# Zeros under the low parts of the keys: the 64-row products of two attentions take 128 rows

## The chip, the cores and the metric

The kernel runs on one core of a Trainium2 chip. The metric is the time of one launch on the device in microseconds (us). TensorE is called PE below, its loads of the stationary operand PEld; VectorE is DVE, ScalarE ACT, GpSimd POOL, and SP issues most of the DMAs.

## What is computed

Two decoder blocks over 256 tokens of width 2048 in float32. The first has three attentions side by side (sparse A with an indexer, latent B with rotated key parts, C over a memory), the second a gated recurrence, a convolution and a feed forward. What the change touches is the indexer's score and the rotated part of B's logits; cut from the reference:

```python
def first_block(x, mem, positions, rel_bias, ...):
    h = rms_norm(x, norm_g[l])
    (aq, ak, av, az, iq, ik, iw, bcq, bckv, bkpe, bz, cq, cz, gates) = jnp.split(h @ w_in[l], IN_OFFSETS, axis=-1)
    ...
    iq = iq.reshape(bsz, seq, IDX_HEADS, IDX_DIM)              # 16 heads of 64; ik: 64 wide, one for all heads
    o_a = dsa_attention(aq, ak, av, iq, ik, iw, positions, rel_bias)   # the indexer's relu(iq . ik) picks 64 keys
    ...
    qb = jnp.concatenate([qb[..., :B_NOPE], apply_rope(qb[..., B_NOPE:], cos, sin)], axis=-1)   # 8 heads of 128 + 64
    kb = jnp.concatenate([kb[..., :B_NOPE], apply_rope(kb[..., B_NOPE:], cos, sin)], axis=-1)
    o_b = mla_attention(qb, kb, vb)                            # logits = qb . kb over 128 + 64
```

## The kernel before

**Exact products in pieces.** A number is held as a high part rounded to the type that PE takes in one pass (fp32r) and a low part that is the exact rest. A weight product is three products: high by high, low by high (both with the weights' high part, lines 292 and 293) and high by low (line 295). Weights arrive in chunks of two k tiles (512 KB); ACT makes the high part `wh` (line 277), DVE the low part `wl` (line 278), three chunks ahead of the products, and each chunk is 12 products of 512 columns on PE.

**One order for all.** The order of every engine is fixed when the program is built. `drive` (line 297) walks through the chunks, and after each chunk `side` (line 226) lets the generators of the attentions go one step. So the side work's products stand on PE between two chunks, and its vector work on DVE and ACT between two splits. How many steps a chunk gets is set by costs added up in `debt`, by the helpers `act`, `tt`, `ts`, `mm` and so on; a call straight to an engine adds nothing there.

**The indexer** (`gen_index`, line 752). Heads are 64 wide, so a query's high part lies on rows 0 to 63 of a tile `iqT` and its low part on rows 64 to 127. The key tile `ikT` has two planes: plane 0 has the key's high part twice (rows 0 to 63 and 64 to 127), plane 1 its low part on rows 0 to 63. One product over 128 rows with plane 0 gives high by high and low by high together; a second one over 64 rows adds high by low (lines 801 and 802):

```python
                    self.mm(p[:, i, :], x, ikt[:, 0, :ns], True, False)
                    self.mm(p[:, i, :], x[0:64], ikt[0:64, 1, :ns], False, True)
```

It runs for 16 heads and two token tiles: eight groups of two heads with 256 keys (four products between two chunks), then four groups of four heads with 128 keys (eight products).

**The rotated part of B** (`gen_B_half`, line 958, once for each half of the heads). `qn` and `kn` are the 128 plain channels in float32, one product in two recorded passes; `qp` holds the rotated query's high and low part, `kp` the rotated key's high part twice, `kpl` its low part on rows 0 to 63 (lines 1039 to 1041):

```python
                        self.mm(L[:, j, :ns], qn[:, h, c], kn[:, h, :ns], True, False)
                        self.mm(L[:, j, :ns], qp[:, h, c], kp[:, h, :ns], False, False)
                        self.mm(L[:, j, :ns], qp[0:64, h, c], kpl[0:64, h, :ns], False, True)
```

A group is two heads of one token tile: per half two groups with 128 keys and two with 256, in `attend` (line 412).

The functions, with the line numbers of the profile:

Of the kernel before, what the change touches and what calls it, by code (L numbers as in the profile page):

```python
# [9 lines left out]
F32 = mybir.dt.float32  # L10
# [10 lines left out]
NEG = 1e30  # L21
# [5 lines left out]
KG = 2        # k tiles of a weight chunk  # L27
RAW = 4       # weight chunks in flight from DRAM
LA = 3        # chunks split ahead of the products
NSLOT = 31    # 4 KiB slots  # L30
# [5 lines left out]
def thresholds():  # L36
    """Smallest distance of each T5 bucket."""
    return [0 if b == 0 else (b if b <= 16 else math.ceil(16 * 8 ** ((b - 16) / 16) - 1e-9))
            for b in range(32)]


def shape_constants():
    """Tables that depend on shapes alone."""
    c = {}
    c["k_ident"] = np.eye(P, dtype=np.float32)
    t = np.arange(P)
    tri = np.where(t[None, :] <= t[:, None], 0.0, -1.0).astype(np.float32)
    c["k_causal"] = np.concatenate([tri, np.zeros((P, P), np.float32), tri], 1)
    lev = []
    for i in range(7):  # L50
        lev.append(((t[:, None] >> (i + 1)) == (t[None, :] >> (i + 1)))
                   & ((t[:, None] >> i) != (t[None, :] >> i)))
    c["k_levels"] = np.stack(lev, 1).astype(np.int32)
    thr = np.array(thresholds(), np.float32)
    thr[0] = -NEG
    k5 = np.zeros((P, 8), np.float32)
    k5[:, 0] = np.tile(thr, 4)
    for b in range(4):
        k5[32 * b:32 * b + 32, 1 + b] = 1.0
    c["k_bucket"] = k5  # L60
    inv = np.float32(1) / np.power(np.float32(10000), np.arange(0, 64, 2, dtype=np.float32) / np.float32(64))
    c["k_freq"] = np.tile(inv.astype(np.float32)[None], (P, 1))
    return c


class Slots:
    """Hands out 4 KiB pieces of SBUF by hand."""
# [24 lines left out]
class Job:  # L92
    """One column block of a product: out[256 tokens, n] = x @ w[:, n0:n0+n]."""
# [8 lines left out]
class Builder:  # L102
# [56 lines left out]
    def mm3(self, out, a, b, start=True, stop=True):  # L159
        """(ah + al)^T (bh + bl) without the part below float32's last bit."""  # L160
        self.mm(out, a[0], b[0], start, False)
        self.mm(out, a[1], b[0], False, False)
        self.mm(out, a[0], b[1], False, stop)

    def split(self, hi, lo, src, g=None):
        """hi + lo = src (times g per partition), exactly."""
        if g is None:
            self.act(hi, src)
            self.tt(lo, src, hi.bitcast(F32), ALU.subtract)
        else:  # L170
            self.act(hi, src, AF.Copy, scale=g)
            self.stt(lo, src, g, hi.bitcast(F32), ALU.mult, ALU.subtract)
# [22 lines left out]
    def rstd(self, out, ss, width):  # L195
        """out = (ss / width + eps) ** -0.5, on a few columns."""
        n = self.cols(ss)
        t = self.work([P, 16], "rs_t", bufs=4)[:, :n]
        self.ts(t, ss, 1.0 / width, EPS, ALU.mult, ALU.add)
        self.debt["g"] += 2.0  # L200
        self.nc.gpsimd.tensor_tensor(out, t, self.cneg[:, :n], op=ALU.pow)  # L201

# [41 lines left out]
    def plan(self):  # L244
        """Cuts the jobs into weight chunks."""
        self.chunks, self.raws, self.whs, self.nd, self.ns = [], {}, {}, 0, 0
        for j in self.jobs:
            ks = j.ks
            for c in range(0, len(ks), KG):
                part = ks[c:c + KG]  # L250
                assert part == list(range(part[0], part[0] + len(part)))
                self.chunks.append((j, c // KG, part, c == 0, c + KG >= len(ks)))

# [28 lines left out]
    def products(self, i, outs, tiles):  # L282
        """The chunk's products for some token tiles."""
# [13 lines left out]
    def drive(self):  # L297
# [20 lines left out]
        # the last chunks, one token tile after the other  # L318
# [8 lines left out]
    def gen_T(self, src, hi, lo, g=None, ev=None, free=(), nk=4, pause=False):  # L327
        """Transposes token-major [128, nk*128] pairs into hi + lo, times g per channel."""
# [34 lines left out]
    def hilo(self, nk, name):  # L363
        """hi and lo parts of x^T, four k tiles to a slot."""
        hs = [self.slots.get([P, 4, 256], F32R, f"{name}h{i}") for i in range(nk // 4)]
        ls = [self.slots.get([P, 4, 256], F32R, f"{name}l{i}") for i in range(nk // 4)]
        return hs, ls
# [5 lines left out]
    def head_ss(self, out, src, groups, width):  # L373
        """out[128, groups] = sums of squares of src[128, groups, width]."""
        sq = self.work([P, 768], "sq", bufs=1)[:, :groups * width].rearrange("p (g w) -> p g w", g=groups)
        self.act(sq, src, AF.Square)
        self.red(out, sq)

# [1 line left out]
    def attend(self, rounds):  # L380
# [30 lines left out]
        def s3(r):  # L411
            pt, nst = r.pop("PT"), r["ns"] // P
            if r["dv"] == 256:   # in two parts where the rows are long enough to gain from it
# [44 lines left out]
    def constants2(self):  # L458
        """Everything small that is not needed at once."""
# [53 lines left out]
        # causal masks of the indexer's scores  # L513
# [3 lines left out]
        self.ts(self.causal, self.causal, NEG)     # 0 or -NEG from here on  # L517
        yield 1
        # rope: angle = k * 2 pi + r with |r| <= pi, in exact parts
# [24 lines left out]
        # tables with the norm's gains: out = x * ct + swapped x * sw  # L544
# [14 lines left out]
        # positions relative to the first, exact in float32  # L559
# [14 lines left out]
        # pos_t - threshold, for (t % 4, bucket) on partitions and t // 4 along  # L574
# [5 lines left out]
        # differences of neighbouring buckets' biases, block diagonal over t % 4  # L580
# [13 lines left out]
    def warm(self):  # L594
        """Keeps the tensor engine's clock up until the first operands are in; gets ScalarE's table."""
# [14 lines left out]
    def gen_in(self, src, name, g0, r, hs, ls, at, every):  # L610
        """Loads a [256, 2048] input and transposes it, times the norm's gain; r = its rstd."""
# [32 lines left out]
    def gen_cT(self, blk, tag, g, dst, ev):  # L644
        """Heads' norm of one block (2 heads of 256) and its transpose, in two parts."""
# [60 lines left out]
    def gen_bias(self):  # L706
        """bias[t, h, s] from steps at the buckets' thresholds: 16 tokens' rows (t, h) at a time."""
# [4 lines left out]
        # through DRAM the rows change from (t, h) on partitions to t on partitions  # L712
        dram = [self.pd.tile([8 * P, P * (i + 1)], F32, name=f"biasd{i}", tag=f"biasd{i}") for i in range(2)]

        def steps(u):
            """0/1 steps of 4 or 2 groups of 16 tokens, two of their four parts to a tile."""
# [35 lines left out]
    def gen_index(self):  # L752
# [11 lines left out]
        # rows 0-63 and 64-127: hi and lo of the queries; hi twice, and lo, of the keys  # L764
        ikt = sl.get([P, 2, 256], F32R, "ikT")
        self.act(ikt[:, 0, :], p[:, :256])
# [23 lines left out]
        for tt in (1, 0):  # L790
# [6 lines left out]
            def s0(r):  # L797
                p = self.ps().rearrange("p (j s) -> p j s", j=nh)
                for i, h in enumerate(r["h"]):
                    x = iqT[h // 4][:, (h // 2) % 2, h % 2, tt * P:(tt + 1) * P]  # L800
                    self.mm(p[:, i, :], x, ikt[:, 0, :ns], True, False)
                    self.mm(p[:, i, :], x[0:64], ikt[0:64, 1, :ns], False, True)
# [21 lines left out]
        # the 64 largest of each row, ties to the lower index  # L824
# [14 lines left out]
    def gen_head128(self, blk, nh, dst, g, off=0):  # L839
        """Norm over heads of 128 and transpose: blk [128, 2, .] -> dst[128, nh, 256] times g."""  # L840
# [27 lines left out]
    def gen_A(self):  # L868
# [12 lines left out]
        # rows outside the selection go far below the others  # L881
# [26 lines left out]
    def gen_lat(self):  # L908
        """Transposed latents, and the rotated shared key part."""
# [48 lines left out]
    def gen_B_half(self, half, ct, sw, bc):  # L958
# [3 lines left out]
        # rotated parts: hi and lo of a query's head on rows 0-63 and 64-127; of the keys hi twice, and lo  # L962
# [34 lines left out]
        kpl = sl.get([P, 4, 256], F32R, "bkpl")  # L997
        for i in range(2):
# [33 lines left out]
        for i in range(2):  # L1032
            for t in range(2):
                def logits(L, i=i, t=t):
                    ns = P * (t + 1)
                    for j in range(2):
# [4 lines left out]
                        self.mm(L[:, j, :ns], qp[0:64, h, c], kpl[0:64, h, :ns], False, True)  # L1041
# [8 lines left out]
    def block1(self):  # L1050
# [12 lines left out]
        def begin():  # L1063
            self.warm()
            next(gmem)          # transposes
            self.gains0()
            next(gmem)          # first half
# [165 lines left out]
        # residual  # L1233
# [23 lines left out]
    def x_next(self, x, cb, ssp, r, store, g, name):  # L1257
        """After a residual block: sums of squares, the transposed parts for the next product."""
# [19 lines left out]
    # The lower bounds of the gates are c - c[0:1] over the layers; with one layer that is zero by  # L1278
    # shape, which leaves log f = log_sigmoid(z) and k = 1 - f = sigmoid(-z).
    def gen_hgrn(self, hf):  # L1280
# [4 lines left out]
        # -log f = L - min(z, 0) and -log k = L + max(z, 0), L = log(1 + exp(-|z|)); L passes through Q and K  # L1285
# [51 lines left out]
        # the diagonal  # L1337
# [18 lines left out]
        for li in range(8):  # L1356
# [21 lines left out]
            else:  # L1378
# [4 lines left out]
                for t in range(2):   # keys of tile 1 - t, queries of tile t  # L1383
# [271 lines left out]
    def finish(self, t):  # L1655
        """The last norm of one token tile."""
# [58 lines left out]
```

## Time and profile before

| | |
|---|---|
| timed runs | 2283.58, 2286.21, 2288.13 us; median 2286.21 |
| profiled execution | span 2284.2 us from first to last instruction; no other time of it is given |
| PE busy | 2259.6 us (99% of the span), 10514 products |
| PEld busy | 1882.4 us (82%), as many loads |
| DVE, ACT, POOL busy | 1317.7 us (58%), 1106.9 us (48%), 367.7 us (16%) |
| 16 DMA engines | 58.1% of their time on the main queue, 181 GB/s |
| granted clock of PE | 0.996 of 2.4 GHz over the span |

A busy PE is not PE at its peak: a product's recorded end is modelled, and products overlap in the pipe. What a product costs is read from the distance between its start and the next one's start.

### The profile page before, as it was taken

What the parts mean: (1) busy time and instruction counts of PE and PEld (TensorE: products, weight loads), DVE (VectorE), ACT (ScalarE), POOL (GpSimd) and SP (SyncE); (2) the same over time, 40 slices, a digit from 0 to 9 for tenths busy, and PEclk for the clock granted to TensorE, in tenths of its full rate; (3) what the DMA queues carried; (4) which work ended last, traced back from release to release, by engine and by line L of the source; (5) the groups of instructions that cost most, each with busy time, mean ns of one, the idle gap of its engine ahead of it and who ended that gap; (6) DMA issues with size and microseconds to landing.
All of it is one profiled execution on the core that took longest, in us unless ns stands there. A gap on an engine that the chain in (4) does not pass through costs nothing.

```text
span 2284.2 us, 27699 instructions
## 1 busy us (share of the span) xinstructions
PE 2259.6 (99%) x10514; PEld 1882.4 (82%) x10514; DVE 1317.7 (58%) x1457; ACT 1106.9 (48%) x1410; POOL 367.7 (16%) x299
## 2 busy tenths in 40 slices
PE   9989999999999999999999999999999999999998
PEld 7878878888888888888888888888888888888886
DVE  5744657655756555555675786555445544545545
ACT  5634535555655454444554654544444433444434
POOL 2093102200404101000263352000000000000001
PEclk9999999999999999999999999999999999999999
DMA  8545546555655556566655555566666666666664
GB/s 275 185 150 184 164 134 184 174 167 171 188 156 177 166 175 194 185 202 197 194 161 157 166 169 160 185 187 186 193 187 191 187 192 196 209 192 188 190 193 140
DMA packets 214933, 413.99 MB, mean 181 GB/s; under 512 B 13538, under 2 KB 20304, under 8 KB 214800
## 3 DMA queue, kind: packets, MB, share of 16 engines
q1 hardware_dynamic: 211936, 405.98, 58.1%
q0 software_dynamic: 2256, 5.19, 0.7%
q8 instruction: 82, 1.34, 0.2%
q10 hardware_dynamic: 608, 1.06, 0.1%
q14 instruction: 51, 0.42, 0.0%
HBM read 408.51 MB, written 3.67 MB: 180 GB/s over the span
## 4 chain that ended last, share of the span: by engine, by line
PE 77%; issue 14%; POOL 1%; DMA 0%; ACT 0%; DVE 0%; ACTq 0%; POOLq 0%; DVEq 0%
PE acc L292 24%; PE acc L293 23%; PE acc L295 23%; PE sp L157 4%; PE sp L177 2%; DMA gf<-in_final_norm_w_dram 0%; POOL x L132 0%; POOL bpt L132 0%; POOL ho L132 0%; ACT x L128 0%; DVE x L132 0%; POOL bpe L132 0%; POOL rs L201 0%; ACT zs L128 0%; ACT wh L277 0%
## 5 line engine op out<-in xcount | busy, mean ns | idle before, releaser
L278 DVE TENSOR_TENSOR wl<-raw,wh 128x1024 fp32r<-128x1024 f32 (+4 forms) x765 | 982.3, 1292 | 807.1 <-ACT wh L277 802.5
L277 ACT ACTIVATE wh<-raw 128x1024 fp32r<-128x1024 f32 (+4 forms) x765 | 801.1, 1053 | 873.8 <-PE acc L293 846.0
L292 PE MATMUL acc<-wh,xh 128*128 128x512 f32 (+2 forms) x864 | 342.2, 396 | 0.0
L293 PE MATMUL acc<-wh,xl 128*128 128x512 f32 (+2 forms) x864 | 336.6, 390 | 0.0
L292 PE MATMUL acc<-wh,h3h 128*128 128x512 f32 x704 | 274.8, 390 | 0.0
L293 PE MATMUL acc<-wh,h3l 128*128 128x512 f32 x704 | 273.9, 389 | 0.0
L295 PE MATMUL acc<-wl,xh 128*128 128x512 f32 (+2 forms) x864 | 230.3, 388 | 0.0
L292 PE MATMUL acc<-wh,h2h 128*128 128x512 f32 x512 | 202.2, 395 | 0.0
L293 PE MATMUL acc<-wh,h2l 128*128 128x512 f32 x512 | 199.4, 390 | 0.0
L295 PEld LDWEIGHTS acc<-wl,xh 128*128 128x128 f32 x864 | 162.6, 188 | 32.9
L292 PEld LDWEIGHTS acc<-wh,xh 128*128 128x128 f32 x864 | 162.9, 189 | 32.4
L293 PEld LDWEIGHTS acc<-wh,xl 128*128 128x128 f32 x864 | 163.0, 189 | 30.9
L295 PE MATMUL acc<-wl,h3h 128*128 128x512 f32 x704 | 188.2, 389 | 0.0
L295 PEld LDWEIGHTS acc<-wl,h3h 128*128 128x128 f32 x704 | 132.1, 188 | 27.4
L293 PEld LDWEIGHTS acc<-wh,h3l 128*128 128x128 f32 x704 | 132.2, 188 | 27.2
L292 PEld LDWEIGHTS acc<-wh,h3h 128*128 128x128 f32 x704 | 132.2, 188 | 27.1
L295 PE MATMUL acc<-wl,h2h 128*128 128x512 f32 x512 | 136.9, 389 | 0.0
L292 PE MATMUL acc<-wh,ah 128*128 128x512 f32 x344 | 134.0, 390 | 0.0
L293 PE MATMUL acc<-wh,al 128*128 128x512 f32 x344 | 133.8, 389 | 0.0
L295 PEld LDWEIGHTS acc<-wl,h2h 128*128 128x128 f32 x512 | 96.1, 188 | 20.0
L293 PEld LDWEIGHTS acc<-wh,h2l 128*128 128x128 f32 x512 | 96.2, 188 | 18.9
L292 PEld LDWEIGHTS acc<-wh,h2h 128*128 128x128 f32 x512 | 96.2, 188 | 18.9
(459 smaller groups left out, 2801.1 us busy)
## 6 DMA issues: line engine op xcount, KB each, us to landing
raw<-in_w_in_dram SPq DMA_DIRECT2D x328, 512.0 KB, 3.7
raw<-in_w_gate_up_dram SPq DMA_DIRECT2D x176, 512.0 KB, 4.2
raw<-in_w_down_dram SPq DMA_DIRECT2D x88, 512.0 KB, 4.2
raw<-in_w_out_dram SPq DMA_DIRECT2D x64, 512.0 KB, 4.2
raw<-in_w_branch_dram SPq DMA_DIRECT2D x48, 512.0 KB, 4.0
raw<-in_w_mem_kv_dram SPq DMA_DIRECT2D x31, 512.0 KB, 4.7
raw<-in_w_in_dram SPq DMA_DIRECT2D x8, 464.0 KB, 3.4
raw<-in_w_in_dram SPq DMA_DIRECT2D x8, 448.0 KB, 3.5
```

The source lines that it names most:

```text
L157: self.nc.tensor.matmul(out, lhsT, rhs, start=start, stop=stop)
L177: self.nc.tensor.transpose(out, in_, self.ident if k == P else self.ident[:k, :k])
L277: self.nc.scalar.activation(wh[:, k], r[:, k], AF.Copy)
L278: self.nc.vector.tensor_tensor(wl[:, k], r[:, k], wh[:, k].bitcast(F32), op=ALU.subtract)
L292: self.nc.tensor.matmul(outs[t], a, wh[:, kk], start=first and kk == 0, stop=False)
L293: self.nc.tensor.matmul(outs[t], b, wh[:, kk], start=False, stop=False)
L295: self.nc.tensor.matmul(outs[t], a, wl[:, kk], start=False, stop=last and kk == len(ks) - 1)
```

## The change

Of the comments only their text is gone. Three things change in the program:

```diff
@@ gen_index
         ikt = sl.get([P, 2, 256], F32R, "ikT")
+        self.nc.vector.memset(ikt[64:128, 1, :].bitcast(F32), 0.0)
         self.act(ikt[:, 0, :], p[:, :256])
         self.tt(ikt[0:64, 1, :], p[0:64, :256], ikt[0:64, 0, :].bitcast(F32), ALU.subtract)
@@ gen_index, s0
                     self.mm(p[:, i, :], x, ikt[:, 0, :ns], True, False)
-                    self.mm(p[:, i, :], x[0:64], ikt[0:64, 1, :ns], False, True)
+                    self.mm(p[:, i, :], x, ikt[:, 1, :ns], False, True)
@@ gen_B_half
         kpl = sl.get([P, 4, 256], F32R, "bkpl")
+        self.nc.vector.memset(kpl[64:128].bitcast(F32), 0.0)
         for i in range(2):
@@ gen_B_half, logits
                         self.mm(L[:, j, :ns], qp[:, h, c], kp[:, h, :ns], False, False)
-                        self.mm(L[:, j, :ns], qp[0:64, h, c], kpl[0:64, h, :ns], False, True)
+                        self.mm(L[:, j, :ns], qp[:, h, c], kpl[:, h, :ns], False, True)
```

The second product of a head now streams a key plane of 128 rows, whose lower 64 rows are zero, against the whole query tile. The zeros are written once for the indexer and once for each half of B. Every engine's order stays as it was, but for these three writes on DVE. The first, in the indexer (`iw` are the heads' weights, `wl` the splits of the weight chunks):

```order
 L137 TENSOR_SCALAR iw<-mA 128x32
 L278 TENSOR_TENSOR wl<-raw,wh 128x1024 x2
+L766 MEMSET ikT 64x256
 L132 TENSOR_TENSOR ikT<-sp,ikT 64x256
 L278 TENSOR_TENSOR wl<-raw,wh 128x1024
```

It comes just ahead of the write of the low part. In B it stands further ahead, on DVE before the first key norm of a half (`ss` are the sums of squares of the keys' heads, `rs_t` goes to POOL for the power, `bkn` and `bkpl` are the key tiles; numbers in names differ since there is one instruction more):

```order
 L132 TENSOR_TENSOR bqp<-sp,bqp 64x256 x2
-L146 TENSOR_REDUCE ss_5203<-sq 128x4
-L132 TENSOR_TENSOR ss_5203<-ss_5203,skpe 128x4
-L137 TENSOR_SCALAR rs_t<-ss_5203 128x4
+L999 MEMSET bkpl 64x1024
+L146 TENSOR_REDUCE ss_5205<-sq 128x4
+L132 TENSOR_TENSOR ss_5205<-ss_5205,skpe 128x4
+L137 TENSOR_SCALAR rs_t<-ss_5205 128x4
 L278 TENSOR_TENSOR wl<-raw,wh 128x1024 x5
 L137 TENSOR_SCALAR bkn<-sp,vT 128x512
 L132 TENSOR_TENSOR bkpl<-sp,bkp 64x256 x2
```

Only the line of the zeros is new there; what stood behind stands one instruction later. It is the same in the second half.

## Rows read from the trace of the kernel before

**Rows 1.** The page's head and part 1: busy us (share of span) xinstructions.

```profile
span 2284.2 us, 27699 instructions
...
PE 2259.6 (99%) x10514; PEld 1882.4 (82%) x10514; DVE 1317.7 (58%) x1457; ACT 1106.9 (48%) x1410; POOL 367.7 (16%) x299
```

**Rows 2.** Who PE waited for, whole span: total us, times, longest us.

```profile
PE sp L177 <- POOL cq L132: 4.0, 2, 3.5
```

**Rows 3.** Instructions on tiles ikT and bkpl: ns min/median/max, first and last start, forms.

```profile
L157 PE MATMUL sp<-ikT,iqT x64: 220/328/385, 279.7 to 336.4; 128*128 128x256 f32 x16, 64*128 64x256 f32 x16, 128*128 128x128 f32 x16, 64*128 64x128 f32 x16
...
L132 DVE TENSOR_TENSOR ikT<-sp,ikT x1: 405/405/405, 248.2 to 248.2; 64x256 fp32r<-64x256 f32 x1
...
L157 PE MATMUL sp<-bkpl,bqp x16: 324/352/384, 635.6 to 778.7; 64*128 64x128 f32 x8, 64*128 64x256 f32 x8
```

**Rows 4.** Timeline of PE, indexer, 256 keys: start us, us, instruction, shapes, count.

```profile
279.68 1.21 PE L157 MATMUL sp<-ikT,iqT 128*128 128x256 f32 x4
...
281.16 0.40 PE L293 MATMUL acc<-wh,xl 128*128 128x512 f32 x1
```

**Rows 5.** Timeline of PE and PEld behind that group.

```profile
280.83 0.50 PE L292 MATMUL acc<-wh,xh 128*128 128x512 f32 x1
280.82 0.19 PEld L292 LDWEIGHTS acc<-wh,xh 128*128 128x128 f32 x1
```

**Rows 6.** Timeline of PE and PEld, C's logits: twelve 128-row products, 256 columns.

```profile
261.82 0.28 PE L157 MATMUL sp<-ckT1h,cqT1h 128*128 128x256 f32 x1
...
263.14 0.19 PEld L292 LDWEIGHTS acc<-wh,xh 128*128 128x128 f32 x1
...
263.49 0.40 PE L293 MATMUL acc<-wh,xl 128*128 128x512 f32 x1
```

**Rows 7.** Timeline of PE, indexer, 128 keys.

```profile
334.74 2.01 PE L157 MATMUL sp<-ikT,iqT 128*128 128x128 f32 x8
...
337.02 0.39 PE L293 MATMUL acc<-wh,xl 128*128 128x512 f32 x1
```

**Rows 8.** Timeline of PE, B's logits with 128 keys, one group of two heads.

```profile
635.18 0.38 PE L157 MATMUL sp<-bkn,bqn 128*128 128x128 f32 x2
...
636.87 0.40 PE L293 MATMUL acc<-wh,xl 128*128 128x512 f32 x1
```

**Rows 9.** Timeline of PE, B's logits with 256 keys, one group of two heads.

```profile
642.10 0.59 PE L157 MATMUL sp<-bkn,bqn 128*128 128x256 f32 x2
...
644.44 0.40 PE L293 MATMUL acc<-wh,xl 128*128 128x512 f32 x1
```

**Rows 10.** Timeline of PE, A's logits: two float32 products of 128, then of 256 columns.

```profile
444.25 0.60 PE L157 MATMUL sp<-akT,aqT 128*128 128x128 f32 x4
...
444.93 0.40 PE L293 MATMUL acc<-wh,ucl 128*128 128x512 f32 x1
...
450.61 1.02 PE L157 MATMUL sp<-akT,aqT 128*128 128x256 f32 x4
...
451.70 0.40 PE L293 MATMUL acc<-wh,xl 128*128 128x512 f32 x1
```

**Rows 11.** Chain that ended last, in order of time: start, us, what.

```profile
631.06 1.53 PE sp L177 x14
```

**Rows 12.** Busy time by engine in a stretch: us, PE, PEld, DVE, ACT, POOL, PEclk, DMA.

```profile
279.00:315.00 36.00, 36.00 (x161) 27.42 (x160) 22.29 (x33) 16.70 (x22) 0.00 (x0) 1.00 0.47 140
```

**Rows 13.** Groups by line on DVE: a write of a constant; busy us, mean ns.

```profile
L597 DVE MEMSET warm<- 128x512 f32 x1 | 0.5, 485 | 0.1
```

**Rows 14.** Timeline of DVE, POOL and PE where B's second half makes its keys.

```profile
731.32 4.34 DVE L278 TENSOR_TENSOR wl<-raw,wh 128x1024 fp32r<-128x1024 f32 x3
...
734.54 2.72 POOL L132 TENSOR_TENSOR bpe<-kr,rs 128x128 f32<-128x128 f32 x2
...
736.78 1.07 PE L295 MATMUL acc<-wl,uah 128*128 128x512 f32 x4
...
740.41 0.60 PE L177 MATMUL sp<-ident,ukv 128*128 128x128 f32 x4
```

## The prediction

> **What bounds the kernel now.** I read the page's first part first: PE is busy 2259.6 of 2284.2 us [rows 1]. Next, whom PE waited for: eight entries over the whole span, the largest 4.0 us behind POOL [rows 2], and none of them in the stretches that the change touches. In the indexer PE is busy for all of its 36.00 us while DVE has 22.29 and ACT 16.70 [rows 12]. So PE sets the pace, and what a product costs has to be read from the starts on PE's timeline, since recorded ends overlap. The forms on the two key tiles then give the number of products that change: 32 in the indexer and 16 in B, 48 in all, 24 of 256 columns and 24 of 128 [rows 3].
>
> I measure each group of side products in one way: from its first start to the start of the second weight product (line 293) behind it. That takes in what the group does to the first weight product after it.
>
> - Indexer, 256 keys: 128 and 64 rows in turn, four products. 281.16 - 279.68 = 1.48 us [rows 4].
> - Attention C's logits: twelve products of the same 256 columns and the same type, all over 128 rows. 263.49 - 261.82 = 1.67 us [rows 6].
>
> A weight product of 512 columns takes about 0.23 us from start to start when nothing is in its way, so C's twelve cost 1.67 - 0.23 = 1.44 us, **0.12 us each**. The indexer's four cost 1.48 - 0.23 = 1.25 us, 0.31 each. Half of the four have half the rows, and they run at well under half the speed. C's products also add up three times into one PSUM region, so that is not what slows the indexer's. What differs is the change between 128 and 64 rows. The trace shows how: behind the group the load of the next stationary operand starts at 280.82 and its product at 280.83 [rows 5]. The load is not done ahead, during the product before, and its own product starts with it. Behind C's products the same load starts at 263.14, and the product it belongs to only 0.12 us later, 0.23 before 263.49 [rows 6]. So each step between 64 and 128 rows, in either direction, empties the pipe, and the exposed load and the emptying are paid 48 times on the way in and 48 times on the way out.
>
> **The change, part by part.**
>
> *The indexer with 256 keys, eight groups.* All products are now over 128 rows, the form of C's, so I take C's 0.12. A group then costs 4 x 0.12 + 0.23 = 0.71 us instead of 1.48: 0.77 us less, 8 times, **6.2 us**.
>
> *The indexer with 128 keys, four groups of eight products.* Before: 337.02 - 334.74 = 2.28 us [rows 7]. The trace has no fp32r product of 128 columns over 128 rows in a run of its own. From above the 0.12 of 256 columns bounds it; from below its half, 0.06, if columns alone counted. Nearest are the transposes, also 128 columns behind a load each: 14 in 1.53 us [rows 11], 0.11 us each. I take 0.11, because the load of the stationary operand has the same 128 columns in each case. A group is then 8 x 0.11 + 0.23 = 1.11 us: 1.17 less, 4 times, **4.7 us**.
>
> *B with 128 keys, four groups (two heads each).* Before: 636.87 - 635.18 = 1.69 us [rows 8]. The float32 part stays; A's logits have two such products alone, 444.93 - 444.25 = 0.68 us with the 0.23 [rows 10]. Two 128-row products for each of two heads add 4 x 0.11. After: 0.68 + 0.44 = 1.12, 0.57 less, 4 times, **2.3 us**.
>
> *B with 256 keys, four groups.* Before: 644.44 - 642.10 = 2.34 us [rows 9]. After: 451.70 - 450.61 = 1.09 [rows 10], plus 4 x 0.12 = 0.48, makes 1.57: 0.77 less, 4 times, **3.1 us**.
>
> *The zeros.* Three writes on DVE, over 64 partitions. DVE wrote 512 columns in 485 ns [rows 13]; in proportion that is 0.24 us for the 256 columns of `ikT` and 0.97 us for the 1024 of `bkpl`, 2.2 us in all. I cost them at nothing on the path. The indexer's low part, just behind its zeros, is written at 248.2, and the first product that reads it starts at 279.7 [rows 3]. In B two things are queued behind the zeros on DVE. One is the weight splits: that of 731.32 is one of three in 4.34 us, done about 1.2 us later, and PE takes it at 736.78 [rows 14], some 4.2 us to spare. The other is the keys' norm, which POOL waits for: its last step ends at 734.54 + 2.72 = 737.26 and PE transposes the keys at 740.41 [rows 14], 3.1 us to spare. Both exceed 0.97 us. If that cover were gone, the three writes would cost 2.2 us. A wait of the writes on an older user of their slots costs nothing either: the zeros come ahead of work that POOL itself waits for, so they can only wait for what POOL had done before.
>
> *Who is late next.* Over the 36 us of [rows 12] PE gets some 6 us faster; DVE then has 22.3 of about 30 us and ACT 16.7, and DMA, at 0.47 of its time, moves the same bytes in five sixths of the time. None comes to its limit, so what PE saves reaches the end. Later waits of PE, on POOL and on splits, follow PE's own pace, and no side chain with a wait spans one of the changed groups.
>
> **Sum.** 6.2 + 4.7 + 2.3 + 3.1 = 16.3 us, against the span of 2284.2: 2267.9. The execution that was profiled has only its span as a time; the median of the runs lies 2.0 us above it, and I take the same for the changed kernel: 2286.2 - 16.3 = **2269.9 us**. With 0.06 for the 48 products of 128 columns the saving is 18.7, with 0.12 it is 15.8, and with all zeros on the path as well 13.6.
>
> **The rivals.**
>
> *Nothing changes (the rows are not the cause).* If the 0.31 us came from the operands or from the place in the program, the 128-row form would cost what the 64-row form does, and with the zeros hidden the time stays at 2286. For it speaks that the 128-row products in the same groups are as slow as the 64-row ones. Against it: C's twelve, with the same type, columns and accumulation, and B, where other tiles show the same excess. The Trainium skill, page "TensorE: Matmul & The Clock Gate", section "Why this matters for your kernels", says that a single product over 32 rows takes the time of one over 128; by that rule alone this change would give 2286. The rule holds for a lone product and leaves out what the step between two row counts costs, which [rows 5] show here.
>
> *Slower: time goes with the rows.* If a 64-row product were cheap for its rows and a second half of rows were paid again, each of the 48 would double: 24 x 0.31 + 24 x 0.26 = 13.7 us more (0.26 is (2.28 - 0.23) / 8 from [rows 7]), 2299.9 us. The place is PE's stream of these groups, and it decides from the point where a 128-row product in an unbroken run costs more than 0.31 or 0.26 us. C's cost 0.12, so little speaks for it. The Trainium skill, page "TensorEngine Tiling (Array Packing)", section "Theoretical Speedup", promises up to a factor of two for a contraction of 64 rows or less, which would speak against the change; it needs two such products side by side, and all 48 here sit on rows 0 to 63, one after the other.
>
> *Half of the gain is given back.* PE comes sooner to the next chunk and waits for its split, or for POOL's key norm. From a saving of 16.3, a new wait of 0.5 us behind each of 16 of the 20 groups leaves 8: 2278 us. Against it stand the 4.2 and 3.1 us to spare above.
>
> **How the numbers follow.** Forecast 0.92, half given back 0.03, no change 0.03, slower 0.02. About 0.2% (4.6 us) is what a measurement of this kernel can tell from no change. Both of the first two are faster than that: 0.95; same 0.03; slower 0.02. The range goes from the largest saving (18.7) less the 2.6 us by which the fastest run lies under the median, 2265.0, to the smallest (13.6) plus the 1.9 us of the slowest run, 2274.5; the rivals outside it hold less than 2 in 10.
>
> **What would show it.** Right: four-product groups of the indexer at 0.71 us and eight-product groups at 1.11 by the same measure; all their products 128 rows; loads ahead of their products again; B's groups at 1.12 and 1.57; zeros of 0.24 and 0.97 us on DVE, and no new entry in PE's list of waits. Wrong: the products still 0.26 to 0.31 us apart, a wait of PE behind a split or POOL near 616 or 740 us, or an unchanged span with shorter groups.

## The result: 2269.9 us, 0.7% faster

The changed kernel takes 2269.93 us (median, 2268.29 to 2271.32) against 2285.64 us before (2283.58 to 2288.13): a ratio of 0.9933, 95% interval [0.9921, 0.9945], or 15.7 us less. The forecast was 2269.9 us within 2265.0 to 2274.5. The profiled execution spans 2266.4 us; its run took 2268.29 us, so 1.9 us lie around the span.

The page of the kernel after, head and part 1, answers to [rows 1]:

```profile
span 2266.4 us, 27702 instructions
...
PE 2243.3 (99%) x10514; PEld 1877.0 (83%) x10514; DVE 1318.7 (58%) x1460; ACT 1106.0 (49%) x1410; POOL 368.8 (16%) x299
```

The number of products is the same; PE is busy 16.3 us less, as much as the forecast's sum. DVE has three instructions more and is busy 1.0 us longer. The products on the two key tiles, as in [rows 3], now have no form with 64 rows:

```profile
L157 PE MATMUL sp<-ikT,iqT x64: 220/278/362, 278.5 to 324.7; 128*128 128x256 f32 x32, 128*128 128x128 f32 x32
...
L157 PE MATMUL sp<-bkpl,bqp x16: 275/277/282, 623.6 to 761.7; 128*128 128x128 f32 x8, 128*128 128x256 f32 x8
...
L766 DVE MEMSET ikT<- x1: 272/272/272, 247.2 to 247.2; 64x256 f32 x1
```

The timeline of PE and PEld after, for the same four kinds of group, in the order of [rows 4, 7, 8, 9], with the first load behind the first group:

```profile
278.47 0.64 PE L157 MATMUL sp<-ikT,iqT 128*128 128x256 f32 x4
...
278.82 0.19 PEld L292 LDWEIGHTS acc<-wh,xh 128*128 128x128 f32 x1
...
278.94 0.40 PE L292 MATMUL acc<-wh,xh 128*128 128x512 f32 x1
279.17 0.40 PE L293 MATMUL acc<-wh,xl 128*128 128x512 f32 x1
...
312.97 1.00 PE L157 MATMUL sp<-ikT,iqT 128*128 128x128 f32 x8
...
314.10 0.40 PE L293 MATMUL acc<-wh,xl 128*128 128x512 f32 x1
...
623.31 0.38 PE L157 MATMUL sp<-bkn,bqn 128*128 128x128 f32 x2
...
624.43 0.40 PE L293 MATMUL acc<-wh,xl 128*128 128x512 f32 x1
...
629.66 0.59 PE L157 MATMUL sp<-bkn,bqn 128*128 128x256 f32 x2
...
631.22 0.40 PE L293 MATMUL acc<-wh,xl 128*128 128x512 f32 x1
```

From the first start to the second weight product the groups take:

| group | count | before | forecast | after | saved, all groups |
|---|---|---|---|---|---|
| indexer, 256 keys | 8 | 1.48 | 0.71 | 0.70 | 6.2 |
| indexer, 128 keys | 4 | 2.28 | 1.11 | 1.13 | 4.6 |
| B, 128 keys | 4 | 1.69 | 1.12 | 1.12 | 2.3 |
| B, 256 keys | 4 | 2.34 | 1.57 | 1.56 | 3.1 |

That is 16.2 us. Behind the group the load now starts at 278.82, ahead of its product at 278.94; before, both started together [rows 5].

The two profiled spans differ by 17.8 us. Some 1.2 us of that are not of the change: the first touched group starts at 278.47 instead of 279.68, since PE waited 3.1 us instead of 4.0 for POOL's `cq` far ahead of it and a little less for the first operands. PE's waits after, the same eight entries; the largest answers to [rows 2]:

```profile
PE sp L177 <- POOL cq L132: 3.1, 2, 2.4
...
PE acc L292 <- ACT wh L277: 1.7, 1, 1.7
...
PE sp L177 <- DMA ident<-in_k_ident_dram: 0.9, 1, 0.9
```

No wait of PE behind a split or behind POOL is new, so the zeros stay covered: the work queued behind them is done before PE needs it. The tightest place is the keys' norm in B's second half, where POOL's last step ends at 720.97 + 2.72 = 723.69 and PE transposes it as the second of two, at about 726.37:

```profile
720.97 2.72 POOL L132 TENSOR_TENSOR bpe<-kr,rs 128x128 f32<-128x128 f32 x2
...
726.26 0.38 PE L177 MATMUL sp<-ident,bpe 128*128 128x128 f32 x2
```

That leaves 2.7 us behind one write of zeros. Over the indexer's stretch PE stays busy throughout while the other engines move closer to it, as in [rows 12]:

```profile
279.00:315.00 36.00, 36.00 (x190) 30.89 (x190) 25.74 (x36) 19.54 (x25) 0.00 (x0) 1.00 0.55 175
```

DVE went from 22.29 to 25.74 of 36 us, DMA from 0.47 to 0.55. No engine is at its limit, so the time saved reaches the end.

### The profile page after: what moved, and what is told of

It reads as the page before. It is cut to its first block, busy times and chain, and to the rows that moved or that the text cites. A ratio compares the mean times of both kernels' runs of the same rounds, so it can differ in the third digit from the quotient of the medians.

```text
span 2266.4 us, 27702 instructions
## 1 busy us (share of the span) xinstructions
PE 2243.3 (99%) x10514; PEld 1877.0 (83%) x10514; DVE 1318.7 (58%) x1460; ACT 1106.0 (49%) x1410; POOL 368.8 (16%) x299
## 4 chain that ended last, share of the span: by engine, by line
PE 77%; issue 15%; POOL 1%; DMA 1%; ACT 0%; DVE 0%; ACTq 0%; POOLq 0%; DVEq 0%; SPq 0%
PE acc L292 23%; PE acc L293 23%; PE acc L295 23%; PE sp L157 4%; PE sp L177 2%; DMA xres<-in_x_dram 0%; DMA gf<-in_final_norm_w_dram 0%; POOL x L132 0%; ACT wh L277 0%; POOL ho L132 0%; POOL bpt L132 0%; ACT x L128 0%; POOL bpe L132 0%; DVE wl L278 0%; POOL rs L201 0%
```

## Experiments

Two questions stayed open after the result. Is it the step between row counts that cost, or are a 64-row product or these key tiles slow by themselves? And is the writing of zeros free, or was it only small?

### Each place alone

The indexer's products over 128 rows, B's as before; and the other way round:

```diff
 # e1_index_only, against the changed kernel
-        self.nc.vector.memset(kpl[64:128].bitcast(F32), 0.0)
-                        self.mm(L[:, j, :ns], qp[:, h, c], kpl[:, h, :ns], False, True)
+                        self.mm(L[:, j, :ns], qp[0:64, h, c], kpl[0:64, h, :ns], False, True)
 # e2_b_only, against the changed kernel
-        self.nc.vector.memset(ikt[64:128, 1, :].bitcast(F32), 0.0)
-                    self.mm(p[:, i, :], x, ikt[:, 1, :ns], False, True)
+                    self.mm(p[:, i, :], x[0:64], ikt[0:64, 1, :ns], False, True)
```

> The indexer's second products take 128 rows, B's stay at 64. If each place pays for its own steps between 64 and 128 rows, the indexer's twelve groups alone give 8 x 0.77 + 4 x 1.14 = 10.7 us: about 2274.9 us, ratio to the kernel before 0.9953. The groups then read 0.71 and 1.13 us, B's stay at 1.69 and 2.34 us. If the gain came from one place, or from the start of the kernel (where the two profiles also differ by over 1 us), it is either all 15.7 us (2269.9) or none (2285.6).

> Only B's third products take 128 rows, the indexer's stay at 64. If each place pays for its own steps, B's eight groups give 4 x 0.57 + 4 x 0.78 = 5.4 us: about 2280.2 us, ratio 0.9976, and with the indexer alone the two sum up to the whole change. If B's products hide behind something else, or the zeros of 0.91 us twice are on the path, it is 0 to 3.6 us.

Measured: the indexer alone 2275.33 us, ratio 0.9952 [0.9939, 0.9964]; B alone 2279.55 us, ratio 0.9973 [0.9961, 0.9984]; the kernel before, beside them, 2285.99 us. That is 10.7 us less, as expected, and 6.4 us less where 5.4 were expected (ratio 0.9976, within the interval). Together 17.1 us against 15.7 for the whole change; the intervals are some 2.6 us wide to either side, so within them the two add up. The traces say it more sharply: the groups save 10.8 us in the first kernel and 5.4 in the second, 16.2 together as in the whole change. The timeline of PE in the first kernel shows a group of the indexer in its short form and a group of B in its long one:

```profile
279.25 0.64 PE L157 MATMUL sp<-ikT,iqT 128*128 128x256 f32 x4
...
279.96 0.40 PE L293 MATMUL acc<-wh,xl 128*128 128x512 f32 x1
...
624.10 0.38 PE L157 MATMUL sp<-bkn,bqn 128*128 128x128 f32 x2
...
625.79 0.40 PE L293 MATMUL acc<-wh,xl 128*128 128x512 f32 x1
```

0.71 and 1.69 us. In the second kernel it is the other way round: the indexer's groups read 1.48 and 2.28 us, B's 1.12 and 1.56. Each place pays for its own steps, and neither gives back anything to the other.

### Still 64 rows, but fewer steps

No zeros, 64 rows as in the kernel before. Only the order within a group changes: the 64-row products stand together at its end. The whole group also becomes one accumulation, which its first product starts and its last one ends.

```diff
 # e3_runs_of_64, against the kernel before
-                    self.mm(p[:, i, :], x, ikt[:, 0, :ns], True, False)
-                    self.mm(p[:, i, :], x[0:64], ikt[0:64, 1, :ns], False, True)
+                    self.mm(p[:, i, :], x, ikt[:, 0, :ns], i == 0, False)
+                for i, h in enumerate(r["h"]):
+                    x = iqT[h // 4][:, (h // 2) % 2, h % 2, tt * P:(tt + 1) * P]
+                    self.mm(p[:, i, :], x[0:64], ikt[0:64, 1, :ns], False, i == nh - 1)
...
-                        self.mm(L[:, j, :ns], qn[:, h, c], kn[:, h, :ns], True, False)
+                        self.mm(L[:, j, :ns], qn[:, h, c], kn[:, h, :ns], j == 0, False)
                         self.mm(L[:, j, :ns], qp[:, h, c], kp[:, h, :ns], False, False)
-                        self.mm(L[:, j, :ns], qp[0:64, h, c], kpl[0:64, h, :ns], False, True)
+                    for j in range(2):
+                        ...
+                        self.mm(L[:, j, :ns], qp[0:64, h, c], kpl[0:64, h, :ns], False, j == 1)
```

> No zeros and 64 rows as before; only the order within a group changes: first all 128-row products, then all 64-row ones, in one accumulation group. If the step between row counts is what costs, a group has two steps instead of 4 (four products of the indexer, B) or 8 (eight products): groups of 1.48 - 0.39 = 1.09 us, 2.28 - 0.86 = 1.42, 1.69 - 0.29 = 1.41 and 2.34 - 0.39 = 1.95 us, 9.2 us less in all: 2276.4 us, ratio 0.996. Within a run of 64-row products the starts lie 0.11 to 0.12 us apart. If a 64-row product is slow by itself, or the key tiles are, nothing changes: 2285.6 us. If time went with rows, a 64-row product in a run would take half of 0.12 us and the saving would be larger, up to 12 us.

Measured: 2277.71 us, ratio 0.9959 [0.9945, 0.9972], so 8.3 us less by the medians and 9.4 by the ratio, against 9.2 expected. Its timeline of PE, two groups of the indexer and pieces of the run of four 64-row products in the second (its first three, its last three and its last one):

```profile
278.42 0.82 PE L157 MATMUL sp<-ikT,iqT 128*128 128x256 f32 x4
279.18 0.50 PE L292 MATMUL acc<-wh,xh 128*128 128x512 f32 x1
279.51 0.40 PE L293 MATMUL acc<-wh,xl 128*128 128x512 f32 x1
...
316.08 1.15 PE L157 MATMUL sp<-ikT,iqT 128*128 128x128 f32 x8
...
317.49 0.39 PE L293 MATMUL acc<-wh,xl 128*128 128x512 f32 x1
...
316.57 0.55 PE L157 MATMUL sp<-ikT,iqT 64*128 64x128 f32 x3
...
316.73 0.49 PE L157 MATMUL sp<-ikT,iqT 64*128 64x128 f32 x3
...
316.95 0.27 PE L157 MATMUL sp<-ikT,iqT 64*128 64x128 f32 x1
```

The groups take 1.09 and 1.41 us, expected were 1.09 and 1.42. With four steps the first kind took 0.77 us more than without any, with two steps 0.39: 0.19 us for each step. With eight steps the second kind took 1.14 us more, with two 0.28: 0.14 each. The excess goes by the number of steps, not by the number of 64-row products, which is the same as before. The last three rows start with the run's first, second and fourth product: 0.16 us from the first to the second, then 0.22 for two, 0.11 each. So behind its first product the run is as dense as one over 128 rows.

So a 64-row product is neither slow by itself nor cheaper than one over 128 rows. That is read with 128 columns; the runs with 256 columns are only two products long. How much of a step is the load that starts late and how much the emptying, the runs do not separate. The Trainium skill, page "TensorEngine Tiling (Array Packing)", section "Key Properties", says that changing the tiling mode, and not just the tile, drains the engine. With 64 and 128 rows taken as two modes the traces agree, at 0.14 us a step with 128 columns and 0.19 us with 256.

### The same order, all products over 128 rows

```diff
 # e6_runs_of_128: the order of the experiment above, with the zeros and the full tiles
+        self.nc.vector.memset(ikt[64:128, 1, :].bitcast(F32), 0.0)
-                    self.mm(p[:, i, :], x[0:64], ikt[0:64, 1, :ns], False, i == nh - 1)
+                    self.mm(p[:, i, :], x, ikt[:, 1, :ns], False, i == nh - 1)
...
```

> The changed kernel, with the order of the experiment that ran the 64-row products behind the 128-row ones: all products 128 rows, in that order and in one accumulation group. If steps between row counts are all that the order changed there, the order alone changes nothing here: 2269.9 us, ratio 0.993, groups of 0.71, 1.13, 1.12 and 1.56 us. If the order or the single accumulation group gained by itself, it gains here too, up to 9 us: 2261 us.

Measured: 2270.24 us, ratio 0.993 [0.9917, 0.9942]. The order and the single accumulation gain nothing by themselves, and so what they gained with 64 rows was the steps. Its timeline of PE:

```profile
277.30 0.64 PE L157 MATMUL sp<-ikT,iqT 128*128 128x256 f32 x4
277.78 0.40 PE L292 MATMUL acc<-wh,xh 128*128 128x512 f32 x1
278.01 0.40 PE L293 MATMUL acc<-wh,xl 128*128 128x512 f32 x1
```

0.71 us, as in the changed kernel; the other kinds of group take 1.13, 1.12 and 1.57 us.

### More zeros than needed

The changed kernel, with each of B's two writes of zeros made eight and three times:

```diff
 # e4_zeros_x8 (e5_zeros_x3: range(3))
+        for _ in range(8):
-        self.nc.vector.memset(kpl[64:128].bitcast(F32), 0.0)
+            self.nc.vector.memset(kpl[64:128].bitcast(F32), 0.0)
```

> The changed kernel with each of B's two writes of zeros made eight times, 7.3 us on DVE instead of 0.91 at each place. Cover theory: behind one write POOL's key norm ends 3.0 us (first half) and 2.1 us (second half) before PE needs it, so seven more writes, 6.4 us, leave PE waiting 3.4 and 4.3 us: 7.7 us more than the changed kernel, about 2277.6 us, with waits of PE behind POOL's bpe or ukv at about 605 and 726 us. If the writes are free whatever their length, it stays at 2269.9 us; if they were on the path from the first on, it is 12.8 us more: 2282.7 us.

Measured: 2284.48 us (2280.77 to 2289.04), 14.6 us more than the changed kernel, where 7.7 were expected. That there is a cover was right; its size was not, and at the second place its owner was not either. The timelines of DVE and PE and the busy time by engine, at the second place:

```profile
721.25 0.91 DVE L1000 MEMSET bkpl<- 64x1024 f32 x1 [0.27 <-DVE bkpl L1000]
722.43 0.91 DVE L1000 MEMSET bkpl<- 64x1024 f32 x1 [0.27 <-DVE bkpl L1000]
...
726.25 0.39 PE L293 MATMUL acc<-wh,ual 128*128 128x512 f32 x1
731.60 2.08 PE L295 MATMUL acc<-wl,uah 128*128 128x512 f32 x4 [4.96 <-DVE wl L278]
733.47 0.63 PE L292 MATMUL acc<-wh,xh 128*128 128x512 f32 x1
...
731.60:734.40 2.80, 2.80 (x7) 2.24 (x8) 2.80 (x2) 0.00 (x0) 2.72 (x3) 0.50 0.61 183
737.00:745.00 8.00, 8.00 (x40) 6.69 (x38) 6.86 (x10) 4.35 (x8) 3.32 (x2) 1.00 0.73 238
```

Three things were missed. A further write costs 1.19 us from start to start, not 0.91: it writes the same tile and waits 0.27 us for the one before. What PE waits for first is the low part of a weight chunk (`wl`), which stands on DVE behind the writes, and not POOL's key norm. And the wait of 4.96 us is not all: the four products behind it take 733.47 - 731.60 = 1.87 us, 0.47 each instead of 0.23. The granted clock of these 2.8 us is 0.50, the lower level of 1.2 GHz, where it is 1.00, or 2.4 GHz, from 737 on. So PE had been idle for 5 us, and its first products ran at the lower level. In this kernel's list of waits:

```profile
PE acc L295 <- DVE wl L278: 7.3, 2, 5.0
PE sp L177 <- POOL bpe L132: 3.0, 3, 1.7
```

Which wait ends last differs between the places. The steps of POOL's key norm and their transposes on PE, first at the one place and then at the other:

```profile
606.75 2.72 POOL L132 TENSOR_TENSOR bpe<-kr,rs 128x128 f32<-128x128 f32 x2
609.52 0.33 PE L177 MATMUL sp<-ident,bpe 128*128 128x128 f32 x1 [1.00 <-POOL bpe L132]
...
733.55 2.72 POOL L132 TENSOR_TENSOR bpe<-kr,rs 128x128 f32<-128x128 f32 x2
737.18 0.38 PE L177 MATMUL sp<-ident,bpe 128*128 128x128 f32 x2
```

At the first place PE waits 2.4 us for `wl`, goes on at the lower clock, and then waits another 1.2 us for the norm, whose last step POOL ends at 609.47. There the norm decides how late PE is, as was expected. (Its last two steps took 2.72 us where they take 1.74 in the changed kernel; why is not shown.) At the second place POOL ends at 736.27, and PE, held up by `wl` and the slow products, comes to the norm only at 737.18. There the low part decides.

Start for start of the same product, PE falls behind the changed kernel's profile by 5.7 us at the first place and 6.6 us at the second, 12.3 us in all. The new waits of PE are 7.3 us behind `wl` and, of the 3.0 behind `bpe`, 1.2 that the changed kernel doesn't have: 8.6 us from the unrounded waits. The other 3.7 us are products at the lower clock, 2.1 us at the first place, where they only fill time in which the norm is not done yet, and 1.6 us at the second. The profiled run is the fastest of the ten, with a span of 2278.9 us, 12.5 more than the changed kernel's, so its time is accounted for. The ten runs lie 8 us apart, and why the others take longer stays open.

From this run the cover of the low part behind one write is 8.3 - 2.4 = 5.9 us at the first place and 3.3 us at the second. That makes a sharper test:

> The changed kernel with each of B's two writes of zeros made three times. With eight, each further write took 1.19 us of DVE from start to start, and PE waited 2.4 and 5.0 us for the low part of a weight chunk; so the cover behind one write is 8.3 - 2.4 = 5.9 us at the first place and 8.3 - 5.0 = 3.3 us at the second. Two further writes take 2.4 us, less than both, and less than the 3.0 us that POOL's key norm has to spare at the first place; at the second that norm has 2.1, so PE can wait up to 0.3 us there. Cover theory: 2269.9 to 2270.5 us, ratio 0.993, no wait of PE on wl. If every write costs what DVE spends on it, whatever covers it, it is 4.8 us more: 2274.7 us.

Measured: 2268.99 us (2268.35 to 2269.52), ratio 0.9924 [0.991, 0.9937]. The writes, by line on DVE, the list of PE's waits, in which `wl` doesn't appear, and the key norm at the second place:

```profile
L1000 DVE MEMSET bkpl<- 64x1024 f32 x6 | 5.5, 912 | 1.4 <-DVE bkpl L1000 1.1 <-issue 0.3
...
PE sp L177 <- POOL bpe L132: 1.7, 1, 1.7
PE acc L292 <- ACT wh L277: 1.7, 1, 1.7
...
722.57 2.72 POOL L132 TENSOR_TENSOR bpe<-kr,rs 128x128 f32<-128x128 f32 x2
...
725.50 0.38 PE L177 MATMUL sp<-ident,bpe 128*128 128x128 f32 x2
```

DVE spends 5.5 us on them instead of 1.8 and the time stays. The cover is nearly used up: POOL ends at 725.29, and PE takes the second of the two at about 725.60, 0.3 us later. So the norm, with 2.7 us behind one write, has the smaller cover, not the low part with 3.3. The zeros are free up to the cover. Beyond it PE was late by more than what stood out: with eight writes at the second place 8.3 - 2.7 = 5.6 us stood out of the smaller cover, and PE was 6.6 us late.

## Why the prediction was right

**PE sets the pace.** Right: 16.3 us less of PE's busy time, 15.7 us less time, and no new entry among PE's waits.

**The step between row counts costs, not the rows.** Right. The forecast took it from one pair of rows, a load that starts with its product [rows 5], and from C's products beside the indexer's [rows 4, 6]. Both left room for other causes, the key tiles or the accumulation. The runs of 64-row products closed that: same tiles, same rows, fewer steps, and the excess halved or quartered with their number. That the order and the accumulation did not do it is shown by the same order over 128 rows, which gained nothing.

**0.12 us for 256 columns, 0.11 for 128.** Right. The eight-product group after takes 1.13 us, so (1.13 - 0.23) / 8 = 0.113 us. Taking the transposes [rows 11] as the nearest rows was better than either end: columns alone would have given 0.06, and the saving would have been 18.7 us.

**The float32 part from A's logits.** Right: B's groups, of which it is a term, came out within 0.01 us in both sizes.

**The zeros are hidden.** Right, with 0.27 and 0.91 us measured for 0.24 and 0.97. The list of what they must not exceed was right too, but the 3.1 us of the key norm were read too short. At 740.41 PE transposes what POOL had done earlier [rows 14]; the step that POOL ends at 737.26 is the second of the next two, at about 740.95, so there were 3.7 us to spare (the expectations read 3.0 and 2.1 us behind one write in the same way, for 3.5 and 2.7):

```profile
740.84 0.38 PE L177 MATMUL sp<-ident,bpe 128*128 128x128 f32 x2
```

The 4.2 us of the split stand. In the experiment with eight writes I took the shorter of the two for the one that PE meets first, and that failed: PE's products with the low part, on line 295, stand ahead of the transposes of the keys, so lateness shows there first. At the first place the norm still ended last and set the delay.

**The rivals.** Nothing changes: out, by every row above. Time goes with the rows: out, since a 64-row product in a run costs what a 128-row one does. By the Trainium skill, page "TensorE: Matmul & The Clock Gate", section "Why this matters for your kernels", a single product over 32 rows takes as long as one over 128; the runs of 64-row products agree for 64 rows, at 0.11 us with 128 columns, and it is a rule on the product alone, not on its neighbours. Half given back: out, since no wait of PE is new; 2.7 us of cover were left behind the 0.91 us of one write.

The agreement of the medians to 0.1 us is partly luck: the largest term was sized to 0.01 us a group, but the runs of one kernel differ by 3 to 5 us. The forecast took 16.3 us from a median of 2286.2 us, and measured were 15.7 us less than 2285.6; the two differences cancel. The lower end of the range comes out at 2264.9 us by its own terms, and 2265.0 stands there.

## What to carry to other kernels

Where a product over 64 rows stands between ones over 128, count the steps between the row counts and not the rows saved: here each step cost 0.14 to 0.19 us, more than a whole product of 256 columns, while zeros cost a write that other work hid. If the rows can't be filled, put the short products directly behind one another; that gave over half of the gain here with no zeros. And before hiding work on an engine, list all that is queued behind it and that the bounding engine needs, and keep below the smallest cover: here it was not that of the first thing PE meets. Beyond it the wait was paid, and at the second place half-speed products after it.

## What the runs showed of the hardware

Behind a stall of 5 us PE lost time beyond the stall: the four products after it took 0.47 us each instead of 0.23, with a granted clock of 0.50 over 2.8 us, and PE was 6.6 us late in all. Without the slow products it would have met the key norm about 0.6 us before POOL had it done, so by that estimate some 1.0 of their 1.6 us are a loss of their own. Writes of one tile behind one another on DVE start 1.19 us apart, though each takes 0.91: an instruction that waits for the one just ahead of it on its own engine loses 0.27 us here. A step between 64 and 128 rows costs 0.14 us with 128 columns and 0.19 us with 256, and the load behind it starts together with its product instead of 0.12 us ahead.
